# A dilated convolution on one core: output row pairs 2q computed as one product over all 128 rows of the array

## The chip, the core and the metric

The kernel runs on one core of a Trainium2 chip. The core has a matrix engine (TensorE, in the profile PE), a vector engine (VectorE, DVE), a scalar engine (ScalarE, ACT), a general one (GpSimd, POOL) and a sequencer for transfers (SyncE, SP). Sixteen DMA engines move data between DRAM and the on-chip memory (SBUF), which has 128 partitions; TensorE writes its results into PSUM, eight tiles of 128 x 512 f32. The engines run side by side and wait for each other through semaphores.

The metric is device time in microseconds of one execution. Before the change the median of three runs is 128.29 us (127.92 to 129.2).

## What is computed

The reference is a 3x3 convolution with dilation 2, 16 images, 64 input channels, 128 output channels, 64 x 64 pixels, f32 in and out:

```python
batch, c_in, h, w, c_out, k, dilation = 16, 64, 64, 64, 128, 3, 2
x_pad = np.pad(x, ((0, 0), (0, 0), (pad, pad), (pad, pad)))      # pad = 2
output[b, co] += weight[co, ci, kh, kw] * x_pad[b, ci, kh*2 : kh*2+h, kw*2 : kw*2+w]
```

An output row r needs the input rows r-2, r, r+2. Rows taken in pairs (2p, 2p+1) therefore see the pairs p-1, p and p+1. Call an even pair E_q (rows 4q, 4q+1) and the following one O_q (rows 4q+2, 4q+3), and w0, w1, w2 the weights of the three kernel rows. Then

- output pair 2q = w1 E_q + w2 O_q + w0 O_(q-1) = w1 (E_q + O_q) + (w2 - w1) O_q + w0 O_(q-1)
- output pair 2q+1 = w1 O_q + w0 E_q + w2 E_(q+1) = w1 (E_q + O_q) + (w0 - w1) E_q + w2 E_(q+1)

The term w1 (E_q + O_q) is shared, so five row products are needed for two output pairs, where the plain form needs six. Each row product is three matrix products, one for each kernel column.

## The kernel before, in words

Two images are worked on together, eight pairs of images (`pb` = 0 to 7) in all. Input channels are 64, so image 0 of a pair lies on partitions 0 to 63 and image 1 on partitions 64 to 127 of one f16 tile `x16[pb]` (line 70). The load (line 72) is issued by GpSimd and converts from f32 to f16 on the way. Six such tiles exist; `AHEAD = 5` pairs are loaded ahead. GpSimd adds E_q + O_q into `s16` (`prepare`, line 127), in one instruction for both images.

Work for a pair of images goes in four units (`u`, four quads of rows each, 512 output columns). A unit has three phases (line 171), each with one PSUM tile for each image:

1. w1 over `s16`: three products for each image. ScalarE copies the result to `s32` (line 191).
2. w21 = w2 - w1 and w0 over the odd pairs: six products for each image. VectorE adds `s32` and writes rows of the output tile `o` (line 197).
3. w01 = w0 - w1 and w2 over the even pairs: six products for each image, and the same addition.

Every product of these phases has 64 rows of the array (the 64 input channels of one image); the two images' products are issued alternately, one on each half of the array. The weights are therefore kept twice, on both halves of the partitions (`w16` with its index `u` of two, lines 90 to 100, transposed by TensorE at line 107 and copied to `w_sb` at lines 116 and 118). In unit 0 the w0 term leaves out the first quad and in unit 3 the w2 term leaves out the last one, since there the rows beyond the image are zero.

Order is written out by hand, and each engine runs its own list in order. On GpSimd stand: loads of pair 0 (in two pieces, rows 0 to 36 and 36 to 64) and pair 1, the first sum of pair 0 (rows 0 to 20), loads of pairs 2 to 4, the other sums of pair 0, and then for each pair the load of the pair four further on, where there is one, and the sums of the next pair. Loads of pairs 6 and 7 wait until the tile is free. SyncE issues the stores (line 208): for pair 0 of the images in two halves, for the others one store of 2 MB for each image after unit 3. Six output tiles `o` exist, three pairs' worth.

Of the kernel before, what the change touches and what calls it, by code (L numbers as in the profile page):

```python
# [9 lines left out]
@with_exitstack  # L10
def kernel(
    ctx: ExitStack,
    tc: tile.TileContext,
    x: bass.AP,
    weight: bass.AP,
    dilation,
    out: bass.AP,
):
    nc = tc.nc

    B, CI, H, W = x.shape
    CO, CI_w, KH, KW = weight.shape
    d = 2 if isinstance(dilation, bass.AP) else int(dilation)
    assert CI == CI_w == 64 and CO == 128 and KH == KW == 3 and d == 2
    assert B % 2 == 0 and H == W == 64

    P = 128
    f32 = mybir.dt.float32
    f16 = mybir.dt.float16
    NP = B // 2  # L30
    NK = KH * KW

    NQ = H // 4
    UQ = 4
    NU = NQ // UQ  # L40
    QW = 2 * W
    NB = UQ * QW
    UR = 2 * UQ
    KWS = (1, 0, 2)

    SLOT = {"w0": 0, "w1": 1, "w2": 2, "w21": 3, "w01": 4}
    NS = len(SLOT)

    wpool = ctx.enter_context(tc.tile_pool(name="wpool", bufs=1))
    x16pool = ctx.enter_context(tc.tile_pool(name="x16pool", bufs=6))  # L50
    sumpool = ctx.enter_context(tc.tile_pool(name="sumpool", bufs=3))
    spool = ctx.enter_context(tc.tile_pool(name="spool", bufs=4))
    opool = ctx.enter_context(tc.tile_pool(name="opool", bufs=6))
    cpool = ctx.enter_context(
        tc.tile_pool(name="cpsum", bufs=8, space=bass.MemoryType.PSUM)
    )
    ctx.enter_context(tc.manual_schedule())

    x_pair = x.rearrange("(nb two) c h w -> nb (two c) h w", two=2)


    w32 = wpool.tile([CO, CI * NK], f32, name="w32")
    nc.sync.dma_start(out=w32, in_=weight.rearrange("o i h w -> o (i h w)"))

    x16 = {}
    s16 = {}


    def load(pb, cuts):
        x16[pb] = x16pool.tile([P, H, W], f16, tag="x16", name=f"x16_{pb}")  # L70
        for lo, hi in zip(cuts, cuts[1:]):
            nc.gpsimd.dma_start(out=x16[pb][:, lo:hi], in_=x_pair[pb, :, lo:hi])  # L72

    cuts0 = [0, 20, 36, 52, H]
    AHEAD = 5
    load(0, [0, 36, H])
    load(1, [0, H])


    zero = wpool.tile([P, NB], f16, name="zero")  # L80
    nc.vector.memset(zero, 0.0)  # L81
    ident = wpool.tile([P, P], f16, name="ident")
    make_identity(nc, ident)

    warm = cpool.tile([P, NB], f32, tag="ps", name="warm")
    for _ in range(6):
        nc.tensor.matmul(out=warm, lhsT=zero[:, 0:P], rhs=zero, start=True, stop=True)  # L87


    w16 = wpool.tile([CO, NS * KW, 2, CI], f16, name="w16")  # L90
    w32k = w32.rearrange("o (i k) -> o k i", k=NK)
    for u in range(2):
        nc.scalar.copy(out=w16[:, 0:NK, u, :], in_=w32k)  # L93
    for name, a in (("w21", 2), ("w01", 0)):
        for u in range(2):
            nc.vector.tensor_sub(  # L96
                out=w16[:, SLOT[name] * KW : (SLOT[name] + 1) * KW, u, :],
                in0=w32k[:, a * KW : (a + 1) * KW, :],
                in1=w32k[:, KW : 2 * KW, :],
            )  # L100

    w_sb = wpool.tile([P, NS * KW, CO], f16, name="w_sb")
    for n, name in enumerate(("w1", "w21", "w0", "w01", "w2")):
        ps = cpool.tile([P, NB], f32, tag="ps", name=f"wt{n}")
        k0 = SLOT[name] * KW
        for j in range(KW):
            nc.tensor.matmul(  # L107
                out=ps[:, j * CO : (j + 1) * CO],
                lhsT=w16[:, k0 + j, :, :].rearrange("o t i -> o (t i)"),
                rhs=ident,  # L110
                start=True,
                stop=True,
            )
        dst = w_sb[:, k0 : k0 + KW, :].rearrange("p k o -> p (k o)")
        if n % 2 == 0:
            nc.vector.tensor_copy(out=dst, in_=ps[:, 0 : KW * CO])  # L116
        else:
            nc.scalar.copy(out=dst, in_=ps[:, 0 : KW * CO])  # L118


    def prepare(pb, lo, hi):
        if pb not in s16:
            s16[pb] = sumpool.tile([P, 2 * NQ, W], f16, tag="s16", name=f"s16_{pb}")
        src = x16[pb].rearrange("p (q e r) w -> p q e (r w)", e=2, r=2)
        dst = s16[pb].rearrange("p (q r) w -> p q (r w)", r=2)
        q0, q1 = lo // 4, hi // 4
        nc.gpsimd.tensor_add(  # L127
            out=dst[:, q0:q1], in0=src[:, q0:q1, 0, :], in1=src[:, q0:q1, 1, :]
        )

    prepare(0, 0, 20)
    for pb in range(2, AHEAD):
        load(pb, [0, H])
    for lo, hi in zip(cuts0[1:], cuts0[2:]):
        prepare(0, lo, hi)

    def conv(pb, hb, ps, u, terms):

        p0 = hb * CI
        po = ps.rearrange("p (h w) -> p h w", w=W)  # L140
        n, total = 0, len(terms) * KW
        for name, e, shift in terms:
            for kw in KWS:
                dw = (kw - 1) * d
                lo = max(u * UR, -2 * shift)
                hi = min((u + 1) * UR, 2 * NQ - 2 * shift)
                cl, ch = max(0, -dw), min(W, W - dw)
                q0, q1 = (lo + 2 * shift) // 2, (hi + 2 * shift) // 2
                if e == 2:
                    rhs = s16[pb][p0 : p0 + CI, 2 * q0 : 2 * q1, cl + dw : ch + dw]  # L150
                else:
                    rhs = x16[pb].rearrange("p (q e r) w -> p q e r w", e=2, r=2)[
                        p0 : p0 + CI, q0:q1, e, :, cl + dw : ch + dw
                    ]
                o_ap = po[:, lo - u * UR : hi - u * UR, cl:ch]
                if e != 2:
                    o_ap = o_ap.rearrange("p (q r) w -> p q r w", r=2)
                yield dict(
                    out=o_ap,
                    lhsT=w_sb[p0 : p0 + CI, SLOT[name] * KW + kw, :],  # L160
                    rhs=rhs,
                    start=(n == 0),
                    stop=(n == total - 1),
                )
                n += 1

    def phase(pb, u, terms):
        ps = [cpool.tile([CO, NB], f32, tag="ps", name=f"ps{hb}") for hb in range(2)]
        for pair in zip(*(conv(pb, hb, ps[hb], u, terms) for hb in range(2))):
            for m in pair:  # L170
                nc.tensor.matmul(**m)  # L171
        return ps

    for pb in range(NP):
        o = [
            opool.tile([P, H, W], f32, tag="o", name=f"o{pb}_{hb}") for hb in range(2)
        ]
        ov = [t.rearrange("p (q e r) w -> p q e (r w)", e=2, r=2) for t in o]
        for u in range(NU):
            if u == 1 and pb > 0 and pb - 1 + AHEAD < NP:  # L180
                load(pb - 1 + AHEAD, [0, H])
            if pb + 1 < NP:
                if u == 1:
                    prepare(pb + 1, 0, 36)
                elif u == 2:
                    prepare(pb + 1, 36, H)

            s32 = []
            for hb, ps in enumerate(phase(pb, u, [("w1", 2, 0)])):
                s = spool.tile([P, NB], f32, tag="s32", name=f"s32_{hb}")  # L190
                nc.scalar.copy(out=s, in_=ps)  # L191
                s32.append(s)
            for e, terms in enumerate(
                ([("w21", 1, 0), ("w0", 1, -1)], [("w01", 0, 0), ("w2", 0, 1)])
            ):
                for hb, ps in enumerate(phase(pb, u, terms)):
                    nc.vector.tensor_add(  # L197
                        out=ov[hb][:, u * UQ : (u + 1) * UQ, e, :],
                        in0=ps.rearrange("p (q c) -> p q c", c=QW),
                        in1=s32[hb].rearrange("p (q c) -> p q c", c=QW),  # L200
                    )


            step = NU // 2 if pb == 0 else NU
            if (u + 1) % step == 0:
                fl = slice((u + 1 - step) * 4 * UQ, (u + 1) * 4 * UQ)
                for hb in range(2):
                    nc.sync.dma_start(out=out[2 * pb + hb, :, fl], in_=o[hb][:, fl])
# [35 lines left out]
```

## Time and profile before

| quantity | value |
|---|---|
| runs shown | 127.92, 128.29, 129.2 us; median 128.29 |
| the profiled execution's own time | 127.88 us |
| its span, first to last instruction | 126.1 us |
| TensorE busy | 105.5 us, 981 products |
| products of the three phases (line 171) | 960 |
| VectorE busy | 83.0 us; 128 additions of 683 ns |
| ScalarE busy | 38.9 us; 64 evictions of 589 ns |
| GpSimd busy | 39.7 us; 18 sums of 1915 ns in the mean, 9 loads |
| last product starts its end chain | 110.45 us in the chain of waits |
| DRAM read and written | 17.07 MB and 33.55 MB |

The profile is of one execution, so its durations are compared with its own time, 127.88 us; the 1.8 us beyond the span lie before the first and after the last instruction. A busy share is an average over the span: which work sets the end is read from the slices and from the waits. The profile counts a converting load by the bytes it leaves in SBUF, f16, which is half of what it reads. A product's record is longer than its share of the array's time, as products are pipelined: start-to-start distances tell more than durations.

### The profile page before, as it was taken

Reading aid. Unit: us, or ns where it says so; the run is one execution under the profiler, and the core shown is the slowest. Engines: PE = TensorE matmul, PEld = TensorE weight load, DVE = VectorE, ACT = ScalarE, POOL = GpSimd, SP = SyncE. Lnnn points to the kernel's source line nnn. Section 1 sums busy time; section 2 is a strip of 40 time slices with the busy share of each in tenths; the row PEclk is TensorE's granted clock in tenths of the full one; section 3 lists DMA queues with packets and bytes.
Section 4 is the critical chain, followed back from the end, with each engine's and each line's share of the span. In section 5 each row is a group of like instructions: output and inputs, shape, how many; then the busy total and the mean of one; then the engine's idle time right before and its main releaser. Section 6 shows DMA issues by size and latency. Waiting matters only on the chain.

```text
span 126.1 us, 2411 instructions
## 1 busy us (share of the span) xinstructions
PE 105.5 (84%) x981; PEld 55.6 (44%) x981; DVE 83.0 (66%) x136; ACT 38.9 (31%) x69; POOL 39.7 (31%) x33
## 2 busy tenths in 40 slices
PE   6357999999999999989999999999999999940000
PEld 2043555555555555535555555555555655510000
DVE  0550677787778777289839988777877777770000
ACT  4733133333333333303333333333333333300000
POOL 6129795949429319100930093000000000000000
PEclk9999999999999999999999999999999999998555
DMA  4899999999999999999999999999999999989990
GB/s 107 151 218 214 218 216 198 265 288 268 304 268 289 286 283 289 289 390 421 418 431 442 416 437 421 437 426 421 437 421 431 426 431 426 434 353 416 421 421 16
DMA packets 4042, 42.38 MB, mean 336 GB/s; under 512 B 448, under 2 KB 448, under 8 KB 832
## 3 DMA queue, kind: packets, MB, share of 16 engines
q1 hardware_dynamic: 2736, 33.85, 63.8%
q0 software_dynamic: 1296, 8.39, 32.9%
q8 instruction: 7, 0.11, 0.3%
q14 instruction: 3, 0.02, 0.0%
HBM read 17.07 MB, written 33.55 MB: 402 GB/s over the span
## 4 chain that ended last, share of the span: by engine, by line
PE 79%; DMA 6%; DVE 2%; POOL 1%; issue 1%; DVEq 0%; POOLq 0%
PE ps L171 79%; DMA x<-in_x_dram 6%; DVE o L197 2%; POOL s L127 1%; DVEq L239 0%; DVEq L197 0%; POOLq L225 0%
## 5 line engine op out<-in xcount | busy, mean ns | idle before, releaser
L197 DVE TENSOR_TENSOR o<-ps,s 128x512 f32<-128x512 f32 x128 | 79.3, 683 | 25.2 <-PE ps L171 21.0
L171 PE MATMUL ps<-x,w_sb 64*128 64x496 f16 (+3 forms) x768 | 88.8, 368 | 0.6 <-DVE o L197 0.6
L171 PEld LDWEIGHTS <-w_sb 64*128 64x128 f16 x960 | 53.4, 95 | 50.4 <-issue 5.0
L191 ACT COPY s<-ps 128x512 f32<-128x512 f32 x64 | 34.4, 589 | 67.9 <-issue 52.4
L127 POOL TENSOR_TENSOR s<-x 128x1152 f16<-128x1152 f16 (+4 forms) x18 | 34.0, 1915 | 31.6 <-PE ps L171 13.9
L171 PE MATMUL ps<-s,w_sb 64*128 64x496 f16 (+1 forms) x192 | 29.8, 379 | 2.3 <-POOL s L127 2.3
L72 POOL DMA_DIRECT2D x<-in_x_dram x9 | 5.1, 569 | 5.0 <-PE ps L171 4.2
L87 PE MATMUL warm<-zero 128*128 128x512 f16 x6 | 2.7, 630 | 1.2 <-DVE zero L81 1.2
L107 PE MATMUL wt<-ident,w 128*128 128x128 f16 x15 | 1.8, 312 | 2.2 <-ACT w L93 2.2
L96 DVE TENSOR_TENSOR w<-w 128x192 f16<-128x192 f32 x4 | 1.7, 494 | 2.6 <-DMA w<-in_weight_dram 2.6
L107 PEld LDWEIGHTS <-w 128*128 128x128 f16 x15 | 1.5, 146 | 3.1 <-ACT w L93 3.1
L93 ACT CAST w<-w 128x576 f16<-128x576 f32 x2 | 2.3, 1218 | 1.7 <-DMA w<-in_weight_dram 1.7
L116 DVE CAST w_sb<-wt 128x384 f16<-128x384 f32 x3 | 1.7, 558 | 1.4 <-PE wt L107 1.2
L87 PEld LDWEIGHTS <-zero 128*128 128x128 f16 x6 | 0.7, 137 | 2.3 <-DVE zero L81 1.2
L93 ACT ACT_TABLE_LOAD x1 | 1.3, 1283 | 0.7 <-PEq L225 0.7
L118 ACT CAST w_sb<-wt 128x384 f16<-128x384 f32 x2 | 1.0, 479 | 1.1 <-PE wt L107 1.1
L81 DVE MEMSET zero<- 128x256 uint32 x1 | 0.3, 272 | 0.9 <-PEq L225 0.9
masks.py:199 POOL TENSOR_SCALAR_AFFINE_SELECT ident<-ident 128x128 f16<-128x128 f16 x1 | 0.3, 293 | 0.1
masks.py:197 POOL MEMSET ident<- 128x128 f16 x1 | 0.2, 231 | 0.0
L225 POOL MEMSET const-float32-0.0<- 128x1 f32 x1 | 0.1, 99 | 0.2 <-issue 0.2
L225 POOL MEMSET const-bfloat16-1.0<- 128x1 bf16 x1 | 0.1, 101 | 0.0
L225 POOL MEMSET const-uint8-127<- 128x1 uint8 x1 | 0.1, 101 | 0.0
(1 smaller groups left out, 0.1 us busy)
## 6 DMA issues: line engine op xcount, KB each, us to landing
out_dram<-o SPq DMA_DIRECT2D x14, 2048.0 KB, 17.2
x<-in_x_dram POOLq DMA_DIRECT2D x7, 1024.0 KB, 22.8
out_dram<-o SPq DMA_DIRECT2D x4, 1024.0 KB, 20.2
x<-in_x_dram POOLq DMA_DIRECT2D x1, 576.0 KB, 7.4
x<-in_x_dram POOLq DMA_DIRECT2D x1, 448.0 KB, 8.9
w<-in_weight_dram SPq DMA_DIRECT2D x1, 288.0 KB, 2.9
```

Of the source, the lines that this page charges most:

```text
L72: nc.gpsimd.dma_start(out=x16[pb][:, lo:hi], in_=x_pair[pb, :, lo:hi])
L87: nc.tensor.matmul(out=warm, lhsT=zero[:, 0:P], rhs=zero, start=True, stop=True)
L93: nc.scalar.copy(out=w16[:, 0:NK, u, :], in_=w32k)
L96: nc.vector.tensor_sub(out=w16[:, SLOT[name] * KW : (SLOT[name] + 1) * KW, u, :], in0=w32k[:, a * KW : (a + 1) * KW, :], in1=w32k[:, KW : ...
L107: nc.tensor.matmul(out=ps[:, j * CO : (j + 1) * CO], lhsT=w16[:, k0 + j, :, :].rearrange("o t i -> o (t i)"), rhs=ident, start=True, stop= ...
L116: nc.vector.tensor_copy(out=dst, in_=ps[:, 0 : KW * CO])
L118: nc.scalar.copy(out=dst, in_=ps[:, 0 : KW * CO])
L127: nc.gpsimd.tensor_add(out=dst[:, q0:q1], in0=src[:, q0:q1, 0, :], in1=src[:, q0:q1, 1, :])
L171: nc.tensor.matmul(**m)
L191: nc.scalar.copy(out=s, in_=ps)
L197: nc.vector.tensor_add(out=ov[hb][:, u * UQ : (u + 1) * UQ, e, :], in0=ps.rearrange("p (q c) -> p q c", c=QW), in1=s32[hb].rearrange("p (q ...
L225: nc = _bacc.Bacc("TRN2", target_bir_lowering=False, num_devices=1)
```

## The change

Each image gets a tile of its own with all 128 partitions, `xt[n][hb]`, four pairs of them in turn (`NT = 4`). The image is loaded onto its half of the partitions (image 0 on 0 to 63, image 1 on 64 to 127), with one transfer for each image. ScalarE then copies the odd row pairs O_(q-1) onto the other half, one quad further on, so that at the place of O_q on the image's own half the other half holds O_(q-1). For the first quad VectorE writes zeros there, once at the start.

With that, phase 2 is one product over 128 rows for each image and kernel column: its weights have w2 - w1 on the image's own half and w0 on the other (`SLOT` entries 0 and 1 for the two images). Six products over 128 rows take the place of twelve over 64 in a unit. Phases 1 and 3 stay as they were, with 64-row products in alternation. The products are 768 in all, where there were 960.

What moves with it: sums are two instructions on 64 partitions each; a load of pair pb+3 is issued in unit 1 of pair pb, into the tiles of pair pb-1, and waits for all that read them; the load of pair 3 stands behind the first pair's sums on GpSimd; copies for the next pair stand on ScalarE after the evictions of units 2 and 3 (for pair 0 before and after the first evictions). The weights are prepared in another order, with w1 first. The last pair of images is stored in halves as well.

```diff
-    SLOT = {"w0": 0, "w1": 1, "w2": 2, "w21": 3, "w01": 4}
+    NT = 4
+    SLOT = {"w1": 0, "w01": 1, "w2": 2, 0: 3, 1: 4}
...
+    xt = [
+        [wpool.tile([P, H, W], f16, name=f"x{n}_{hb}") for hb in range(2)]
+        for n in range(NT)
+    ]
...
     def load(pb, cuts):
-        x16[pb] = x16pool.tile([P, H, W], f16, tag="x16", name=f"x16_{pb}")
         for lo, hi in zip(cuts, cuts[1:]):
-            nc.gpsimd.dma_start(out=x16[pb][:, lo:hi], in_=x_pair[pb, :, lo:hi])
+            for hb in range(2):
+                nc.gpsimd.dma_start(
+                    out=xt[pb % NT][hb][hb * CI : (hb + 1) * CI, lo:hi],
+                    in_=x[2 * pb + hb, :, lo:hi],
+                )
...
+    for hb in range(2):
+        nc.vector.tensor_sub(out=half(hb, hb), in0=kh(2), in1=kh(1))
+        nc.scalar.copy(out=half(hb, 1 - hb), in_=kh(0))
...
+    for n in range(NT):
+        for hb in range(2):
+            c = slice((1 - hb) * CI, (2 - hb) * CI)
+            nc.vector.memset(xt[n][hb][c, 2:4], 0.0)
...
+    def sums(pb, lo, hi):
...
+        for hb in range(2):
+            p = slice(hb * CI, (hb + 1) * CI)
+            src = quads(xt[pb % NT][hb])
+            dst = s16[pb].rearrange("p (q r) w -> p q (r w)", r=2)
+            nc.gpsimd.tensor_add(
+                out=dst[p, q0:q1], in0=src[p, q0:q1, 0, :], in1=src[p, q0:q1, 1, :]
+            )
+
+    def copies(pb, lo, hi):
+        q0, q1 = lo // 4, min(hi // 4, NQ - 1)
+        for hb in range(2):
+            t = quads(xt[pb % NT][hb])
+            nc.scalar.copy(
+                out=t[(1 - hb) * CI : (2 - hb) * CI, q0 + 1 : q1 + 1, 1, :],
+                in_=t[hb * CI : (hb + 1) * CI, q0:q1, 1, :],
+            )
+
+    sums(0, 0, 20)
+    load(2, [0, H])
     for lo, hi in zip(cuts0[1:], cuts0[2:]):
-        prepare(0, lo, hi)
+        sums(0, lo, hi)
+    load(3, [0, H])
+    copies(0, 0, 36)
...
+    def even(pb, u):
+        ps = psum()
+        for hb in range(2):
+            for n, kw in enumerate(KWS):
+                co_, ci_ = cols(kw)
+                nc.tensor.matmul(
+                    out=ps[hb].rearrange("p (q r w) -> p q r w", r=2, w=W)[:, :, :, co_],
+                    lhsT=w_sb[:, SLOT[hb] * KW + kw, :],
+                    rhs=rows(pb, hb)[:, u * UQ : (u + 1) * UQ, 1, :, ci_],
+                    start=(n == 0),
+                    stop=(n == KW - 1),
+                )
+        return ps
...
+            if u == 1 and pb > 0 and pb - 1 + NT < NP:
+                load(pb - 1 + NT, [0, H])
+            if pb + 1 < NP and u in (1, 2):
+                sums(pb + 1, *((0, 36) if u == 1 else (36, H)))
...
+            if pb == 0 and u == 0:
+                copies(0, 36, H)
+            if pb + 1 < NP and u in (2, 3):
+                copies(pb + 1, *((0, 36) if u == 2 else (36, H)))
...
-            step = NU // 2 if pb == 0 else NU
+            step = NU // 2 if pb in (0, NP - 1) else NU
```

## The prediction

> **What bounds the kernel now.** I read the totals and the 40 slices first, then the transfer queues, then single microseconds at both ends of the span.
>
> ```profile
> PE 105.5 (84%) x981; PEld 55.6 (44%) x981; DVE 83.0 (66%) x136; ACT 38.9 (31%) x69; POOL 39.7 (31%) x33
> ...
> PE   6357999999999999989999999999999999940000
> ...
> DMA  4899999999999999999999999999999999989990
> GB/s 107 151 218 214 218 216 198 265 288 268 304 268 289 286 283 289 289 390 421 418 431 442 416 437 421 437 426 421 437 421 431 426 431 426 434 353 416 421 421 16
> ...
> q1 hardware_dynamic: 2736, 33.85, 63.8%
> q0 software_dynamic: 1296, 8.39, 32.9%
> ```
>
> TensorE is full from slice 5 to slice 35. But the transfer engines are full from slice 2 to slice 38, and their two queues alone fill 96.7% of the span. GB/s counts a load by the f16 bytes it leaves, half of what it reads: 8.39 MB left are 16.78 MB read. 216 GB/s of loads alone, or 425 GB/s of stores alone, are therefore the same load on the engines: about 0.43 MB of DRAM traffic per us. A pair's load (2.10 MB read) takes 4.9 us of it, a pair's store (4.19 MB) 9.8 us; together 14.7 us, more than TensorE's time for a pair (below). So there are two routes to the end: transfers that never pause, and TensorE followed by the last store.
>
> ```profile
> 18.00:19.00 1.00, 1.00 (x12) 0.55 (x10) 1.00 (x3) 0.30 (x1) 1.00 (x2) 1.00 1.07 221
> ...
> 111.00:112.00 1.00, 0.75 (x9) 0.23 (x4) 1.00 (x3) 0.00 (x0) 0.00 (x0) 1.00 0.84 360
> 112.00:113.00 1.00, 0.00 (x0) 0.00 (x0) 1.00 (x2) 0.00 (x0) 0.00 (x0) 1.00 0.54 229
> 113.00:114.00 1.00, 0.00 (x0) 0.00 (x0) 0.03 (x1) 0.00 (x0) 0.00 (x0) 1.00 1.09 459
> ```
>
> These are single microseconds: after the five engines come the granted clock, the DMA share and GB/s. TensorE ends at 111.75. The transfers dip there (0.16 + 0.46 - 0.09, some 0.5 us): the store backlog had just run out when the last pair was ready. So the two routes end nearly together today. From the last store's issue (113.06 in the timeline) to the end of the span are 13.0 us.
>
> The timeline gives the clockwork of TensorE (start, duration, engine, line):
>
> ```profile
> 14.65 0.81 PE L171 MATMUL ps<-s,w_sb 64*128 64x512 f16 x6
> 15.28 2.71 PE L171 MATMUL ps<-x,w_sb 64*128 64x512 f16 x24
> ...
> 17.82 0.81 PE L171 MATMUL ps<-s,w_sb 64*128 64x512 f16 x6
> ```
>
> One unit takes 17.82 - 14.65 = 3.17 us for 15 pairs of products, 211 ns a pair: the two half-array products of a pair run beside each other. Units 0 and 3 take 3.02 us (20.99 to 24.00), because one term lacks a row pair's quarter at the image's edge.
>
> **The change, part by part.**
>
> *The products.* 192 pairs of 64-row products (w21 and w0) become 192 products over 128 rows. The count falls from 960 to 768, the time slots stay 480. The unit-0 saving at the upper edge goes, since the zeroed rows are now multiplied: 8 x 0.15 = 1.2 us more. A 128-row weight load behind a 128-row product is shown: the 15 weight transposes start 107 ns apart, each with weights of its own. So no weight load is charged.
>
> *The change of shape.* TensorE goes from halves to whole and back in each of 32 units, 64 times. No row shows a switch. The nearest is the step from one tile group to the next, with its waits and other operands, which costs nothing (14.65 to 15.28 is 3 x 211). The far end: the next product waits until the last is out. A product lasts 376 ns by the records against 213 of streaming, 163 ns more, so 64 x 0.163 = 10.4 us; with the following weight load unhidden (95 ns mean) 16.5 us. Below nothing is excluded, since the columns must stream. I take 55 ns a switch, 3.5 us, near the zero row. [...]
>
> *GpSimd.* A sum over 128 partitions becomes two over 64. Elements per partition set the rows (1152: 2369 ns, 896: 1885, 640: 1392, 512: 1181, 384: 932), so I take the same duration for a half; the low end is half of it. A pair's sums then cost 2 x (2369 + 1885) = 8.5 us, and two load issues 2 x 0.55, together 9.6 of 12.5 us: hidden, as they start when the pair before last has ended and are needed 12.5 us later. At the start they are not hidden. Today the first sum runs from 8.74 to 10.13 and TensorE starts at 10.19. Afterwards it needs two: if both pieces land at 8.67 the start is 1.4 later; if the first half's piece lands well earlier it is 0. I take 0.7.
>
> *ScalarE.* Copies per image of 9 x 128 and 6 x 128 elements. Rows: 589 ns for 512 and 479 for 384 give 0.86 ns an element and 0.15 fixed, so 1.14 and 0.81 us. Unit 2: two evictions (1.07) + 2.28 = 3.35 against 3.17 us; unit 3: 2.69. The 0.2 us lag is made up at once: hidden. The far end is the strided cast (1218 ns for 576, 2.1 ns an element): 5.9 + 4.3 against 6.3 us, evictions 3.9 us late, of which the eight PSUM tiles (some 2.5 us of products) hide most; 1.4 us x 7 pairs = 10 us. The low end is nothing. The first copies run from 8.7 to 11.0, before TensorE's first whole-array product.
>
> *Vector.* Eight small memsets (the 128x256 one takes 272 ns, so at most 2.2 us in all), in the idle stretch before the weight evictions, ending by 7.6; the sums wait for data until 8.7. Free.
>
> *Loads.* Same bytes; 18 issues for 9, at 0.53 to 0.69 us on GpSimd's queue. A half's transfer reaches 64 partitions. No row shows such a one: if they are as fast, 0; if the loads alone in the first 19 us ran at half rate, +16 us. The nearest row, a 128-partition load of the same bytes per partition, says 0, taken. [...]
>
> *Four tiles for six: the third load ahead is late.* Image pair 3 is now issued behind the six first sums: GpSimd 10.1 (or 11.5), + 1.1 for pair 2's issues, + 2 x (1.18 + 1.18 + 0.93) = 17.8 to 19.2, and data flow 1.6 us after an issue (1.23 to 2.82 for the first load), at 19.4 to 20.8. Pairs 0 to 2 (3.15 MB left, and 0.4 of weights and code) are through at 19.0: the GB/s of the single microseconds add up to 3.57 MB there. The first store is issued 8.54 us after TensorE's start today (18.73); afterwards + 0.15 + four switches, at 18.9 to 20.7, flowing 0.6 later. So the engines run dry for 0.3 to 2.0 us, **taken 1.2**. From then on work never lacks: first half store and pair 3 last until 30, the second half store (25 to 26.5) and load 4 (issued at 27.4 to 29, behind the second pair's sums and the wait for pair 0's products) until 40, when store 1 and load 5 are there; then 14.7 us of transfers per 12.5 to 13 us of TensorE.
>
> *The last pair in halves.* Only half, 4.9 us, follows TensorE: 13.0 - 4.9 = 8.1 us after the last issue. The dip at 112 goes: 0 to 0.6 less on the transfers (some engines had none); I take 0.3.
>
> **The sum**, from the profiled execution (127.88, of it 126.1 span and 1.8 around). Transfers: 126.1 + 1.2 - 0.3 = **127.0**. TensorE: 111.75 + 1.2 + 0.7 - 0.2 (part of the 0.6 it lost waiting for an output tile) = 113.4; + 1.3 to the last issue (111.75 to 113.06) + 8.1 = 122.8, + 3.5 of switches = 126.3. The later one stands: 127.0 + 1.8 = 128.8. The median of the runs (128.29) is 0.4 above the profiled one: **129.2**. 1% either way, about what a measurement here can tell from none, is 127.0 to 129.6.
>
> **The rivals.**
> 1. *As forecast, transfers bound*: the ends of gap and dip give 128.0 (0.3 and 0.6) to 130.3 (2.0 and 0). Chance 0.38.
> 2. *The switches decide* (0.27): beyond 66 ns each TensorE's route passes 127.0. At 110 ns: 122.8 + 7.0 + 2.2 = 132.0; at 163: 135.4. For it: a product's 163 ns beyond streaming, which a wait for its end would lay open; against it: the free step between groups. Late copies on ScalarE would look alike in the result.
> 3. *The loads slow down* (0.21): 64-partition transfers at 10 to 20% less rate add 1.9 to 4.2 us in the 17 us in which they run alone: 131.1 to 133.4. For it: every load of the trace reaches all 128 partitions, so nothing vouches for a half. Against: what a load writes (216 GB/s) is half of what stores read in the same memory (425), so there is room.
> 4. *Not slower: no gap* (0.14). The first image's half of the first piece lands before the second's, its sum runs in the wait that ends at 8.74 today, TensorE starts at 10.2 as before, load 3 is issued at 17.8 and the first store at 18.9, both within 0.5 us of the 19.0 at which the queue would run dry. Then only the dip's removal stays: 126.1 - 0.6 to 126.1 + 0.3, so, with 2.2 around, 127.7 to 128.6. It decides if the gap is under 0.3 us and a switch under 50 ns.
>
> That TensorE gets shorter, as 960 to 768 suggests, would need pairs that do not overlap; 211 ns a pair excludes it, and with the transfers full it would move nothing.
>
> Faster by over 1%: 0.07 (half of case 4's better end, a sliver elsewhere); within: 0.38 (most of case 1 and of 4); slower: 0.55 (cases 2 and 3 and a third of 1). The range 127.4 to 134.0 leaves out the full drain and the worst copies.
>
> **What would show it.** Transfers: a dent in DMA share near 19 to 21 us and none at 112. Products: 192 whole-array ones 211 ns apart, and the start-to-start step at each change of shape, 211 or more. GpSimd: some 68 us busy; ScalarE: some 65. First unit: TensorE's first product of sums between 10.2 and 11.6. Loads: x GB/s from 3 to 18 us at 216 or less. I am wrong if TensorE's units take over 3.6 us, or if the loads stretch.

## The result

The changed kernel takes 131.83 us (median of six runs, 131.5 to 132.13), the kernel before 128.19 us beside it. The ratio is 1.026, with an interval of 1.022 to 1.030: slower by 3.6 us. The forecast was 129.2 us with a range to 134.0; of its cases, the second one happened, in which the changes of shape on TensorE decide. Some executions of one and the same kernel take 1.5% or more longer than its fastest; the ratios leave them out, and the one profile here that shows such an execution is that of the run with half-array products (131.04 us).

The page of the changed kernel, totals, slices and queues, as shown for the kernel before:

```profile
PE 113.9 (88%) x789; PEld 44.3 (34%) x789; DVE 88.2 (68%) x144; ACT 70.5 (54%) x105; POOL 79.0 (61%) x60
...
PE   6539999999999999999999999999999999995000
...
DMA  4999999999999999999999999999999959999990
GB/s 103 139 203 215 214 204 149 181 360 393 292 280 411 320 320 322 398 378 307 338 363 380 325 335 338 418 443 423 428 433 418 443 247 403 411 421 413 426 413 20
...
q1 hardware_dynamic: 3024, 33.85, 62.3%
q0 software_dynamic: 1440, 8.39, 33.4%
```

The profiled execution took 131.88 us, its span is 130.1. TensorE issues 192 products fewer and is busy 8.4 us longer. The transfer engines have a hole that they did not have before, in slice 32 (5 for 9, 247 GB/s). Single microseconds of it, with the last three columns granted clock, DMA share and GB/s:

```profile
105.00:106.00 1.00, 1.00 (x12) 0.37 (x8) 0.55 (x2) 0.71 (x1) 0.00 (x0) 1.00 0.35 147
106.00:107.00 1.00, 1.00 (x7) 0.51 (x6) 0.85 (x3) 0.83 (x2) 0.00 (x0) 1.00 0.19 82
...
118.00:119.00 1.00, 0.84 (x10) 0.28 (x6) 0.55 (x2) 0.00 (x0) 0.00 (x0) 1.00 0.94 393
```

In the mean of the sixteen engines 0.65 + 0.81 = 1.5 us of transfer time are lost. A transfer reports sixteen completions in the trace; for the last transfer of pair 5's store eleven of them are in by 105.9, and pair 6's store is issued only at 106.21, where it was issued at 100.09 before. Some engines still work through the hole, but the last completions show a loss as well: that of pair 5 comes at 107.84 and that of the next 2.1 MB at 114.43, 6.6 us later, where the 2.1 MB behind those take 4.9 (119.29). From the issue on 8.4 MB, two pairs' stores, have to follow, at about 0.43 MB per us some 19.7 us; their data flows from 107.1 to 128.6. TensorE ends at 118.84 instead of 111.75.

The clockwork of TensorE, one unit and the start of the next in the timeline (start, duration, engine, line; L185 the sums, L203 the whole-array phase, L222 the even pairs):

```profile
15.04 0.80 PE L185 MATMUL ps<-s,w_sb 64*128 64x512 f16 x6
...
15.77 1.44 PE L203 MATMUL ps<-x,w_sb 128*128 128x512 f16 x6
...
17.15 1.44 PE L222 MATMUL ps<-x,w_sb 64*128 64x512 f16 x12
...
18.43 0.80 PE L185 MATMUL ps<-s,w_sb 64*128 64x512 f16 x6
```

Starts are what counts. Three pairs of half products take 15.77 - 15.04 = 0.73 us, where before the same three took 0.63 (14.65 to 15.28): 0.10 more ahead of the first whole-array product. The six whole-array products take 1.38 us for six times 0.211 = 1.27: 0.11 more ahead of the first half product. From the even pairs to the next sums, halves to halves, nothing is added (1.28). In the single records the step from the last product of one shape to the first of the other is 301 or 302 ns into the whole array and 305 or 306 ns out of it, at every change in all units after the first. A step without a change is 205 to 216 ns for products of full width; only the step right behind a change is a little longer, 225 to 227. The unit takes 3.39 us for 3.17.

### The profile page after: what moved, and what is told of

The parts are those of the page before. It is cut to its first block, busy times and chain, and to the rows that moved or that the text cites. A ratio compares the mean times of both kernels' runs of the same rounds, so it can differ in the third digit from the quotient of the medians.

```text
span 130.1 us, 2110 instructions
## 1 busy us (share of the span) xinstructions
PE 113.9 (88%) x789; PEld 44.3 (34%) x789; DVE 88.2 (68%) x144; ACT 70.5 (54%) x105; POOL 79.0 (61%) x60
## 4 chain that ended last, share of the span: by engine, by line
PE 84%; DMA 5%; POOL 2%; issue 1%; DVE 1%; DVEq 0%; POOLq 0%
PE ps L203 35%; PE ps L222 33%; PE ps L185 16%; DMA x<-in_x_dram 5%; POOL s L150 1%; DVE o L255 1%; POOL x L77 1%; DVEq L297 0%; POOLq L150 0%; POOLq L283 0%
## 5 line engine op out<-in xcount | busy, mean ns | idle before, releaser
L255 DVE TENSOR_TENSOR o<-ps,s 128x512 f32<-128x512 f32 x128 | 83.8, 689 | 28.1 <-PE ps L222 17.5
L150 POOL TENSOR_TENSOR s<-x 64x1152 f16<-64x1152 f16 (+4 forms) x36 | 68.6, 1904 | 4.4 <-DMA x<-in_x_dram 1.9
L203 PE MATMUL ps<-x,w_sb 128*128 128x496 f16 (+1 forms) x192 | 47.2, 383 | 0.0
L222 PE MATMUL ps<-x,w_sb 64*128 64x496 f16 (+3 forms) x384 | 44.9, 366 | 0.0
L158 ACT COPY x<-x 64x1152 f16<-64x1152 f16 (+1 forms) x32 | 31.7, 990 | 0.7
L185 PE MATMUL ps<-s,w_sb 64*128 64x496 f16 (+1 forms) x192 | 26.7, 378 | 2.4 <-POOL s L150 2.4
L203 PEld LDWEIGHTS <-w_sb 128*128 128x128 f16 x192 | 16.4, 99 | 28.9 <-issue 14.6
L222 PEld LDWEIGHTS <-w_sb 64*128 64x128 f16 x384 | 16.1, 94 | 27.6 <-issue 13.3
L77 POOL DMA_DIRECT2D x<-in_x_dram x18 | 9.7, 550 | 9.5 <-ACT x L158 8.8
L185 PEld LDWEIGHTS <-w_sb 64*128 64x128 f16 x192 | 9.5, 95 | 13.2 <-issue 2.7
L106 ACT CAST w<-w 128x192 f16<-128x192 f32 x2 | 1.0, 528 | 1.8 <-DMA w<-in_weight_dram 1.8
L110 ACT CAST w<-w 128x192 f16<-128x192 f32 x2 | 1.0, 528 | 0.0
```

Source lines behind the costliest of these rows:

```text
L77: nc.gpsimd.dma_start(out=xt[pb % NT][hb][hb * CI : (hb + 1) * CI, lo:hi], in_=x[2 * pb + hb, :, lo:hi],)
L106: nc.scalar.copy(out=half("w1", u), in_=kh(1))
L150: nc.gpsimd.tensor_add(out=dst[p, q0:q1], in0=src[p, q0:q1, 0, :], in1=src[p, q0:q1, 1, :])
L158: nc.scalar.copy(out=t[(1 - hb) * CI : (2 - hb) * CI, q0 + 1 : q1 + 1, 1, :], in_=t[hb * CI : (hb + 1) * CI, q0:q1, 1, :],)
L185: nc.tensor.matmul(out=ps[hb].rearrange("p (h w) -> p h w", w=W)[:, :, co_], lhsT=w_sb[p, kw, :], rhs=s16[pb][p, u * UR : (u + 1) * UR, ci ...
L203: nc.tensor.matmul(out=ps[hb].rearrange("p (q r w) -> p q r w", r=2, w=W)[:, :, :, co_], lhsT=w_sb[:, SLOT[hb] * KW + kw, :], rhs=rows(pb, ...
```

## The experiments

Two theories were tried. A: the 64 changes of shape make TensorE late, and the stores wait for it. B: loads on half the partitions, late loads and doubled sums cost the time.

**Half-array products in phase 2.** Undo the products alone; tiles, loads, sums, copies and both halved stores stay.

```diff
-        for hb in range(2):
+        for back in range(2):
+            q0 = max(u * UQ, back)
+            q1 = (u + 1) * UQ
             for n, kw in enumerate(KWS):
                 co_, ci_ = cols(kw)
-                nc.tensor.matmul(
+                for hb in range(2):
+                    p = slice(hb * CI, (hb + 1) * CI)
+                    s = SLOT[1 - hb if back else hb] * KW
+                    nc.tensor.matmul(
...
-                    lhsT=w_sb[:, SLOT[hb] * KW + kw, :],
-                    rhs=rows(pb, hb)[:, u * UQ : (u + 1) * UQ, 1, :, ci_],
+                        lhsT=w_sb[p, s + kw, :],
+                        rhs=rows(pb, hb)[p, q0 - back : q1 - back, 1, :, ci_],
...
```

> The changed kernel with its phase 2 alone put back: w21 and w0 again as twelve products on 64 rows, each image on its own half of the partitions, no change of shape in the units; tiles, loads, sums, copies (now read by nobody) and the stores in halves stay as changed. Theory A (64 changes of shape at about 94 ns, the start-to-start steps of 305 and 302 ns in the trace of the changed kernel against 209, are what costs): units 3.17 us again, TensorE ends near 111.5 instead of 119, then transfers set the end: 128.3 to 129.5 us. Theory B (loads on half the partitions, late loads, doubled sums cost the time): no change, 131.3 to 132.2 us.

Ratio to the kernel before 1.0058 (1.0011 to 1.0105), which is 128.8 us beside a kernel before of 128.0 (the seven executions that count took 128.29 to 129.62), where the changed kernel stands at 1.0262. Its timeline (L208 is phase 2):

```profile
31.39 0.99 PE L185 MATMUL ps<-s,w_sb 64*128 64x512 f16 x6
32.02 1.63 PE L208 MATMUL ps<-x,w_sb 64*128 64x512 f16 x12
33.29 1.63 PE L229 MATMUL ps<-x,w_sb 64*128 64x512 f16 x12
34.56 0.79 PE L185 MATMUL ps<-s,w_sb 64*128 64x512 f16 x5
```

34.56 - 31.39 = 3.17 us, and 0.63 us from the sums to phase 2; the profile of the run below that adds an early load (127.78 us) has the same two numbers. So of 2.6% the whole-array products carry 2.0; sums, copies and loads together leave 0.6%. The 2.0 hold two things, the changes of shape and the products over zeroed rows at the upper edge; the next two runs vary the changes alone.

**Whole-array phases side by side.** Even units in the order sums, even pairs, whole; odd units whole, sums, even pairs. (The code names phases after their output rows: `even` is the whole-array phase 2, `odd` is phase 3, over the even pairs.)

```diff
+            first = even(pb, u) if u % 2 else None
             for hb, ps in enumerate(shared(pb, u)):
...
-            for e, terms in enumerate((even, odd)):
...
+            def add(e, psl):
...
+            if u % 2:
+                add(0, first)
+                add(1, odd(pb, u))
+            else:
+                add(1, odd(pb, u))
+                add(0, even(pb, u))
```

> The changed kernel with its phases in another order: in even units sums, even pairs, whole-array phase; in odd units whole-array phase, sums, even pairs, so that two whole-array phases stand side by side. Same products, 32 changes of shape instead of 64. Theory A: 3.0 us less for TensorE, which ends near 116; the end gains 1.5 to 3, 128.9 to 130.4 us. Theory B: 131.3 to 132.2 us.

Ratio 1.0194 (1.0152 to 1.0236), 130.37 us. Here the two phases stand together:

```profile
33.21 2.71 PE L203 MATMUL ps<-x,w_sb 128*128 128x512 f16 x12
35.85 0.81 PE L185 MATMUL ps<-s,w_sb 64*128 64x512 f16 x6
...
115.00:116.00 1.00, 0.47 (x6) 0.09 (x2) 0.94 (x2) 0.51 (x2) 0.00 (x0) 1.00 0.98 410
```

Twelve whole-array products take 2.64 us, 12 x 0.211 and one change. The neighbours are other ones now, even pairs into whole and whole into sums, and the steps are again 301 to 302 and 305 ns: it is the change of shape that sets them, and not a wait for a certain phase's operands. TensorE ends at 115.5, 3.4 us earlier, for 32 changes less. The time gains less, 0.9 us by the ratios, 1.5 by the medians: the hole at 105 is closed (DMA share 0.93 and 1.08 in those two microseconds), and the transfers, at 0.98 to 1.01 from 114 to 118 us, run on past TensorE's end: they are the bound.

**Twice the changes.** Whole-array products of image 0, the w01 products, whole-array products of image 1, the w2 products; the same products in another order.

```diff
...
+        whole(0)
+        halves("w01", 0)
+        whole(1)
+        halves("w2", 1)
...
```

> The changed kernel with phase 2 and 3 interleaved: whole-array products of image 0, the w01 products, whole-array products of image 1, the w2 products. Same products, 128 changes of shape instead of 64. Theory A: every further change costs 94 ns, 6.0 us more for TensorE, which ends near 125; the last store then follows an emptier queue: 135.0 to 138.0 us. Theory B: 131.3 to 132.5 us.

Ratio 1.0779 (1.0722 to 1.0836), 137.65 us: more than the changed kernel by 5.8 us (medians) or 6.6 us (ratios), for 64 changes more. In the timeline every stretch of three slots (0.63 us) that ends in a change takes 0.73 or 0.74; in the single microseconds of the transfers there is now a hole of four, from 108 to 112:

```profile
100.71 0.81 PE L239 MATMUL ps<-x,w_sb 128*128 128x512 f16 x3
101.45 0.81 PE L254 MATMUL ps<-x,w_sb 64*128 64x512 f16 x6
102.19 0.81 PE L239 MATMUL ps<-x,w_sb 128*128 128x512 f16 x3
...
108.00:109.00 1.00, 1.00 (x7) 0.31 (x8) 0.84 (x3) 0.96 (x2) 0.00 (x0) 1.00 0.01 0
...
111.00:112.00 1.00, 1.00 (x7) 0.21 (x3) 1.00 (x2) 0.52 (x2) 0.00 (x0) 1.00 0.00 0
```

With 32, 64 and 128 changes the kernel takes 130.4, 131.8 and 137.7 us: the first step is damped by the transfers, the second costs 5.8 to 6.6 us / 64 = 91 to 104 ns a change, what the records show for one.

**The last pair stored whole again.**

```diff
-            step = NU // 2 if pb in (0, NP - 1) else NU
+            step = NU // 2 if pb == 0 else NU
```

> The changed kernel without the halved last store: image pair 7 is stored whole after unit 3, as before the change. If TensorE's route sets the end (theory A), 4.2 MB instead of 2.1 follow the last product, less what was queued: 133.7 to 135.5 us. If transfers that never pause set it (the forecast's first case), the place of the last issue matters little: 131.5 to 132.5 us.

Ratio 1.0461 (1.0396 to 1.0526), 133.55 us, a little under what A expected (133.7) and far from the other case. The engines pause a second time, ahead of the last store:

```profile
117.00:118.00 1.00, 1.00 (x13) 0.47 (x12) 0.84 (x2) 0.00 (x0) 0.00 (x0) 1.00 0.08 33
118.00:119.00 1.00, 0.26 (x4) 0.00 (x0) 0.71 (x2) 0.00 (x0) 0.00 (x0) 1.00 0.00 0
```

So in the changed kernel the halved store saves 1.7 us by the medians, 2.5 by the ratios.

**The halved last store alone, in the kernel before.** The same line, changed the other way.

```diff
-            step = NU // 2 if pb == 0 else NU
+            step = NU // 2 if pb in (0, NP - 1) else NU
```

> The kernel before with the last image pair stored in halves, nothing else changed. The forecast's term: the dip of the transfers at 112 us goes, 0 to 0.6 us less, 127.6 to 128.2 us. Rival: some of the sixteen engines never paused in the dip, so nothing is won, 128.0 to 128.4 us.

Ratio 1.0029 (0.9990 to 1.0068), 128.09 us: nothing won. The dip is gone,

```profile
112.00:113.00 1.00, 0.90 (x11) 0.33 (x5) 1.00 (x3) 0.00 (x0) 0.00 (x0) 1.00 0.93 393
```

0.93 where it was 0.54, and the time stays. The mean over sixteen engines had shown a pause, but in the packet records of the kernel before never fewer than eight packets were in flight in the two microseconds of the dip, and never fewer than three around it (at 113.25 us). The sixteen completions of each store in that trace show why this was enough. The last three came at 114.08, 114.63 and 115.17 for the store ahead of the pause, at 118.96, 119.50 and 120.04 for the first image of the last pair, at 123.81, 124.36 and 124.89 for the second: 4.85 to 4.88 us from one to the next each time, while the other thirteen were through at 123.64. The completions carry no engine's name, but steps as even as these leave no room for a pause in the part of the work that ends last; the pause lay in engines that had time to spare.

**Loads cut by partitions, in the kernel before.**

```diff
-            nc.gpsimd.dma_start(out=x16[pb][:, lo:hi], in_=x_pair[pb, :, lo:hi])
+            for hb in range(2):
+                nc.gpsimd.dma_start(
+                    out=x16[pb][hb * CI : (hb + 1) * CI, lo:hi],
+                    in_=x[2 * pb + hb, :, lo:hi],
+                )
```

> The kernel before with each load cut into two transfers of 64 partitions each into the same tile; all else unchanged, same bytes. Theory A (a load on half the partitions takes the engines longer: the load queue's packet time is 33.4% of 130.1 us = 43.5 us in the changed kernel against 41.5): the transfers are its bound, so 1 to 2 us more, 129.2 to 130.3 us. Theory B (a half costs nothing, the load queue grew for another reason, such as what stands beside it): 127.7 to 128.6 us.

Ratio 1.0031 (0.9999 to 1.0062), 128.3 us; the load queue's packets take 33.0% of 126.6 us, 41.8 us, as before (41.5). Theory A of this run is wrong: reaching 64 partitions costs no more than 0.6%, most likely 0.3.

**Loads cut by rows, in the kernel before.**

```diff
-            nc.gpsimd.dma_start(out=x16[pb][:, lo:hi], in_=x_pair[pb, :, lo:hi])
+            mid = (lo + hi) // 2
+            for a, b in ((lo, mid), (mid, hi)):
+                nc.gpsimd.dma_start(out=x16[pb][:, a:b], in_=x_pair[pb, :, a:b])
```

> The kernel before with each load cut into two transfers by rows, both over all 128 partitions: as many transfers as in the changed kernel, pieces half as long. If it is the number of transfers that costs (18 instead of 9), as slow as the cut by partitions, 129 to 130.3 us; if it is the reach of 64 partitions, no change: 127.7 to 128.6 us, or a little more for the shorter pieces.

Ratio 1.0121 (1.0077 to 1.0164), 129.63 us. Twice the transfers with half as long pieces (by the edit twice the 1296 packets of the kernel before) cost 1.2%, with a load queue of 34.0% of 127.8 us, 43.5 us; the cut by partitions, also with twice the transfers, costs a quarter of that. The length of the pieces, and with it their number, is what differs.

**Half-array products with the load of pair 3 early.** On top of the first experiment:

```diff
     load(2, [0, H])
+    load(3, [0, H])
     for lo, hi in zip(cuts0[1:], cuts0[2:]):
         sums(0, lo, hi)
-    load(3, [0, H])
```

> The changed kernel with half-array products in phase 2 (128.3 to 129.5 us alone) and the load of image pair 3 moved back to stand beside that of pair 2, ahead of the later sums of pair 0. Theory A (transfers run without a pause except near 18 to 19 us, DMA share 0.47 there in the run with half-array products, so the pause is part of what is left): 0.3 to 0.8 us less than that run. Theory B (the pause is not on the path): no change, within 0.2 us.

Ratio 1.0046 (1.0014 to 1.0078) against 1.0058 (1.0011 to 1.0105): not told apart. The share in the microsecond from 18 to 19 is 0.80 in its profile. How much of a pause the move closed is not shown; nothing of it can be seen in the time.

**Side by side, with earlier loads.** The same move on the order with 32 changes, and the same with `NT = 5` and pairs 3 and 4 loaded early.

```diff
-    NT = 4
+    NT = 5
...
     load(2, [0, H])
+    load(3, [0, H])
+    load(4, [0, H])
```

> The order with whole-array phases side by side (32 changes of shape, 130.4 us, where TensorE ends at 115.5 and the transfers run on without a pause from 20 us to the end) with the load of image pair 3 moved back beside that of pair 2. Theory A (with half the changes gone the transfers are the bound, and their pause near 19 us is what this order has over the kernel before): 0.5 to 1.2 us less, 129.2 to 129.9 us. Theory B (TensorE's route still sets the end): no change or, as the first unit's later sums start 1.1 us later on GpSimd, a little more: 130.2 to 131.2 us.

> The same with five tiles instead of four for the images, and pairs 3 and 4 loaded beside pair 2: loads are then as early as in the kernel before, but for one pair. Theory A, with dearer late loads as a further part (34.0% of 127.9 us = 43.5 us of packet time on the load queue against 41.5 before): 128.4 to 129.4 us, level with the kernel before at best. Theory B: 130.2 to 131.5 us.

Ratios 1.0177 (1.0138 to 1.0216), 130.48 us, and 1.0136 (1.0100 to 1.0172), 129.88 us. The first is what B said. The second lies between the two theories and has the lowest median of the versions that keep the whole-array products, though its interval overlaps the first one's; it is still slower than the kernel before. The slices of the transfers show why, first run, then second:

```profile
DMA  4999999999897999999999999999999999999990
...
DMA  5999999999999999999999999999999949999990
GB/s 104 158 219 211 208 220 226 249 287 287 313 285 326 343 320 310 415 361 333 323 369 436 446 420 410 436 446 425 410 436 446 390 190 436 405 397 423 410 413 13
```

In the first the pause near 19 us is closed (share 0.99), and there are new ones, the larger one in slice 12 (38.6 to 41.9 us, busy for 7 tenths). In the second the hole is back, at 102 to 106 us (190 GB/s in slice 32). Loads that are done earlier leave less work for the engines while TensorE, at some 13 us a pair, is late with the next store.

No version that was run is faster than the kernel before.

## Why the prediction was right in sign and wrong in its likeliest case

**The two routes.** Right as a frame. Half-array products put the changed kernel at 128.8 us, close to the 129.2 that the transfers' route gave, with TensorE's route out of the way. That it is so close is in part luck: of that route's two terms the pause was 0.2 and not 1.2 us in the changed kernel's profile, and the halved last store won nothing in the kernel before instead of 0.3. The changed kernel itself is 3 us above that, in the case to which a chance of 0.27 was given; the range held it, the likeliest value missed it by 2.6 us.

**The change of shape: the step that failed.** "I take 55 ns a switch, 3.5 us, near the zero row." By the records a change costs 93 to 96 ns, and the first product after a change some 10 ns more; a unit grows by 0.21 us, 32 units by 6.7. The choice went by the row that looked nearest, the step between two tile groups of one shape, but that row holds no change of shape. The other end, a wait until the last product is out (the "full drain" of the forecast's range), put at the 163 ns by which a product's record (376 ns) exceeds the 213 ns taken for its streaming (products of 512 columns step by 215 to 216 ns in the trace of the kernel before), was too high: the product after a change starts 67 ns before the recorded end of the last one (22.54 and 22.61 us), an end that is modelled. The forecast's limit was 66 ns a change; at 95 its second case gives 122.8 + 6.1 + 2.2 = 131.1, and the median is 131.83. The runs show that a change costs about 95 ns; what takes this time they do not show. The weight load may have a part in it: inside a phase a weight load starts a slot ahead of its product, at a change only with it (22.54 in the records, 0.30 us after the last half product). Its 92 to 99 ns are about the size of the gap, but in the records they stand at the end of the gap and not in it. No run here shows how large its part is.

**The sum of TensorE's route.** 126.3 us of span were given and 130.1 measured. The changes of shape took 6.7 us for 3.5 (+3.2), the start was 0.9 earlier than taken, the wait for an output tile went whole, 0.6 us where 0.2 was taken off (-0.4), and 9.9 us for 8.1 follow the last issue (+1.8). These make 130.0. The three errors beside the changes cancel to 0.5 us; that the second case at 95 ns comes so close is in part this luck.

**The edge in unit 0.** As worked out: the 3.02 us of unit 0 before is a full unit now, 8 x 0.15 = 1.2 us for TensorE.

**The start.** Taken 0.7 us late, was 0.16 early. The timeline of the changed kernel:

```profile
6.82 1.39 POOL L150 TENSOR_TENSOR s<-x 64x640 f16<-64x640 f16 x1 [1.56 <-DMA x<-in_x_dram]
...
8.59 1.39 POOL L150 TENSOR_TENSOR s<-x 64x640 f16<-64x640 f16 x1 [0.39 <-DMA x<-in_x_dram]
...
10.03 1.41 PE L185 MATMUL ps<-s,w_sb 64*128 64x512 f16 x5 [1.19 <-POOL s L150]
```

The first image's piece lands first, and its sum starts 1.8 us ahead, while the second is on its way, as the fourth case had it.

**The pause near 19 us.** Taken 1.2 us, was 0.2 (shares 0.94 and 0.88). Pair 3's load was issued at 17.80, at the early end of the forecast, and the sixteen completions of pair 2's last piece run from 18.98 to 20.40.

**GpSimd and ScalarE.** Right in the size of one instruction and in being hidden. The rows of the groups (count | busy, mean ns of one | idle before):

```profile
L150 POOL TENSOR_TENSOR s<-x 64x1152 f16<-64x1152 f16 (+4 forms) x36 | 68.6, 1904 | 4.4 <-DMA x<-in_x_dram 1.9
...
L203 PE MATMUL ps<-x,w_sb 128*128 128x496 f16 (+1 forms) x192 | 47.2, 383 | 0.0
...
L158 ACT COPY x<-x 64x1152 f16<-64x1152 f16 (+1 forms) x32 | 31.7, 990 | 0.7
```

A sum over half the partitions takes what a sum over all takes (1904 ns in the mean for 1915), and the copies average 990 ns (1.14 and 0.81 us were worked out, mean 0.98). In busy time 68 us were given for GpSimd, which its sums alone take (68.6); with the load issues it is 79.0. ScalarE has 70.5 for 65; evictions and copies are 66.1 of it, the rest is work on the weights and a table load. Neither is waited for by TensorE after the start: the whole-array phase (L203) has no idle time before it, and the step into it is the same in every unit after the first.

**The last pair in halves.** Mis-sized twice. In the kernel before it is worth nothing (0 to 0.6 was given, 0.3 taken). In the changed kernel 9.9 us, not 8.1, follow the last issue (120.19 to 130.1), since the two stores ahead, from 106.21 on, still fill the queue.

**What stays open.** The load queue's packet time went from 41.5 to 43.5 us. Neither half-partition transfers (41.8) nor the products explain it; it was 42.8 to 44.9 in the five kernels with the late load of pair 3, the changed one among them, and 41.6 and 41.8 in two of the three where pair 3, or 3 and 4, came early, but the third of them had 43.3. The 0.6% that remain with half-array products were not traced to one part.

## What to carry to other kernels

Fewer and larger products are no gain where two half-array products already run side by side: count the slots, not the instructions (here a pair of half products and a whole-array product both take 209 to 216 ns), and look for the bound elsewhere first, here in the transfers. Mixing products on half and on whole row ranges has its own price, here 95 ns for each change; place those of one shape side by side. Where no row shows the price of a change, a row without the change says nothing about it: keep the case in which it decides as a likely one. With two resources this close to the bound, a delay on either one turned into a hole in the other (TensorE's into 1.5 us of lost transfer time in the changed kernel, a wait for stores into 0.6 us on TensorE in the one before), and filling an early hole can open a later one, as in the two versions with earlier loads.

## What was not expected of the hardware

- A step from products on 64 rows to products on 128 rows, or back, takes 301 to 306 ns start to start where it is 205 to 216 without a change; the price is nearly the same in both directions and does not vary between the units after the first.
- A pause in the mean of the sixteen transfer engines (a share of 0.54 for a microsecond) was worth nothing when it was closed: the completions that come last had followed each other without a gap.
- Cutting each load by partitions costs 0.3% (0.0 to 0.6), cutting it by rows, with pieces of half the length, 1.2% (0.8 to 1.6).
